# Round-robin block order in a blocked triangular inverse, one evacuation copy for four blocks, and partition sums on four column strips

## The chip, the cores and the metric

The kernel runs on one core of one Trainium2 chip. The metric is the device time of one execution in microseconds; three executions of the kernel before took 1111.55, 1113.08 and 1113.27 us, median 1113.08 us. TensorE (PE) multiplies, with its weight loads shown apart (PEld); VectorE (DVE), ScalarE (ACT) and GpSimd (POOL) work on vectors; SyncE (SP), ACT and POOL also issue transfers.

## The reference, cut to what matters

One layer of a diffusion backbone over 512 latent tokens and 256 context tokens, width 1024: a modulated norm, one combined input projection, two token mixers side by side (a gated delta rule with four heads and HGRN2 with four heads, each in both directions), an up-projection of each, a gated merge, an output projection and a SwiGLU. The change touches the delta rule's inverse and sums over partitions. In the reference the inverse is a triangular solve for each chunk:

```python
a_mat = jnp.where(strict, beta[..., :, None] * jnp.einsum('bhnid,bhnjd->bhnij', k, k) * decay, 0.0)
rhs = jnp.concatenate([(beta * jnp.exp(g))[..., None] * k, beta[..., None] * v], axis=-1)
sol = lax.linalg.triangular_solve(a_mat, rhs, left_side=True, lower=True, unit_diagonal=True)
...
m_lat = (jax.nn.silu(c) @ mod_w[layer] + mod_b[layer])[:, None, :]
...
return tf * lax.rsqrt(jnp.sum(tf * tf, axis=-1, keepdims=True) + EPS)
```

The last two lines are where sums over partitions come from: the six modulation sections, and the squared norms of queries and keys.

## The kernel before

Weights come in float32, are split into a high and a low part (L92 to L97: a load, an ACT cast `hi`, a DVE subtraction `lo`), and each projection is three products (`mm3`, L105) of 512 or 256 tokens. The mixers are streams: `G0` and `G2` are pairs of delta-rule heads (`gdn_pair`), `H0` to `H3` are HGRN2 heads (`hgrn`), `F` are gate projections used as filler. PLAN (L31) sets the order in which they are emitted; a list scheduler then merges them into one fixed order for each engine, by priority and its own estimates of durations. Each engine runs its list in order. After the delta rule (X in PLAN) its memory is freed, and the loads of the remaining modulation weights (`mwb`, POOL queue, L819) start; then come the up-projections (`pup`), the output projection (`pwo`) and the SwiGLU (`pf`, `pfo`).

The delta rule's inverse (L668 to L757) runs once for each pair of heads. The 128-token chunk is four diagonal 32 x 32 blocks, inverted on DVE (L680 to L685). Then two merging steps, each for e = 0, 1 (the heads of the pair), six chunks g and both directions d:

- 32 to 64: for four blocks (d, b) with rows a and columns z (`quads`), `pR` = N·X (L724), copied to SBUF by ACT (L727), then `pY` = R·Y (L730) and, for two of the blocks, `pX` (L733); ACT copies them into N and X64 (L737, L739).
- 64 to 128: the same with 64 x 64 blocks, two of them: `pRb` (L747), its copy (L750), `pYb` (L753), its copy (L756).

Each product occupies only the 32 x 32 or 64 x 64 block of the PE array that `tile_position` names. The matrices are float32, and the profile shows two PE passes (a weight load and a matmul each) for one such product: L724 has 96 products and 192 passes. All six products of a block are issued one after the other, then the next block.

A sum over partitions is a product of the data as weights [128, 128] with a column of ones: `pn` in `gdn_front` (L623, squared norms: six chunks for keys, four for queries, four heads) and `pmo` in `mod_sum` (L846, two for each of 16 quarter sections). The early modulation sums of `modulation` (L265) have the same form.

Of the kernel before, what the change touches and what calls it, by code (L numbers as in the profile page):

```python
# [13 lines left out]
P = 128  # L14
# [15 lines left out]
# The order in which the streams of the mixers are emitted: name and number of steps; X ends the delta rule.  # L30
# [13 lines left out]
def view(ap, offset, dims):  # L44
    """The tile behind ap, all partitions, with free dimensions given as (step, count)."""
    return bass.AP(ap.tensor, ap.offset + offset, [list(ap.ap[0])] + [list(d) for d in dims])


def body(tc, T, out, tap=None):
# [8 lines left out]
    with ExitStack() as root:  # L58
# [25 lines left out]
        def split(srcs, kt, n, pool=None):  # L84
            """Loads [kt * 128, n] of weights side by side and splits them into two float32r parts."""
            WN[0] += 1
            pool = pool or ring["w"]
            raw = pool.tile([P, kt, n], F32, name=f"raw{WN[0]}", tag="raw", bufs=2)
            c0 = 0
            for s in srcs:  # L90
                w = s.shape[1]
                nc.sync.dma_start(raw[:, :, c0:c0 + w], s.rearrange("(k p) f -> p k f", p=P))  # L92
                c0 += w
            hi = pool.tile([P, kt, n], F32R, name=f"hi{WN[0]}", tag="hi")
            nc.scalar.copy(hi[:, :, :], raw[:, :, :])  # L95
            lo = pool.tile([P, kt, n], F32R, name=f"lo{WN[0]}", tag="lo")
            nc.vector.tensor_tensor(lo[:, :, :], raw[:, :, :], hi.bitcast(F32), op=ALU.subtract)  # L97
            return hi, lo

        def mm3(ps, a, b, kt, start=True, stop=True):  # L100
            """ps += sum_k a_k^T b_k with a, b as (hi, lo) callables of k."""
# [5 lines left out]

        def feat(w, src, n, name, t0=0, tag="mm"):
            """[128 features, n tokens from t0] of the projection with the weights w."""
            ps = bank(tag, name)  # L110
            mm3(ps[:, 0:n], [lambda k, t=t: t[:, k, :] for t in w], [lambda k, t=t: t[:, k, t0:t0 + n] for t in src], KT)
            return ps
# [19 lines left out]
        def gate_low(i, pool):  # L132
            """The same in two halves of the features, out of its own buffers."""
# [15 lines left out]
        with ExitStack() as st:  # L149
# [4 lines left out]
            # small vectors, one row of 128 to a partition: those of the first norm, then the others  # L154
# [71 lines left out]
            def sigmoid_small(dst, src):  # L226
                """1 / (1 + exp(-src)), for the small tiles."""
# [25 lines left out]
            def modulation(d, s):  # L253
                """Shift and scale columns of feature tile d, for the latents (s = 0) or the context (s = 1)."""
# [12 lines left out]
            def mod_columns(s, d0, d1):  # L267
                """The columns of the feature tiles d0 to d1, with the biases and the weight of the norm."""
# [144 lines left out]
        def head_norm(po, gcol, i, on, y, ss, tag, name, eq=None):  # L413
            """po: [128 tokens, 4, 128] -> normalised, scaled by the channel weight, transposed, spilled as row i of ydram."""
# [15 lines left out]
        def hgrn(h):  # L430
            """HGRN2 head, both directions; index 0 of L is the backward one, of K and R the forward one."""
# [19 lines left out]
            for d in range(3):  # L451
# [7 lines left out]
                # softplus(-|z|), then the sigmoids of both signs  # L459
# [100 lines left out]
        def gdn_front(h, res):  # L560
            """Projections and convolution of a Gated DeltaNet head. Queries and keys stay as they are: the norms of the
            keys go into the write strengths and the values, those of the queries into the norm of the output."""
# [9 lines left out]
            for kind, c0 in (("k", 512), ("q", 0), ("v", 1024)):  # L572
# [46 lines left out]
                else:  # L619
                    nc.scalar.activation(acc[:, 0:P * cnt], flat, AF.Square)  # L620
                    pn = bank("ga", m + "pn")
                    for g in range(cnt):
                        nc.tensor.matmul(pn[:, g:g + 1], acc[:, P * g:P * g + P], ones[:, 0:1], start=True, stop=True)  # L623
# [11 lines left out]
        def gdn_pair(h0):  # L635
            """Two Gated DeltaNet heads, both directions."""
# [5 lines left out]
            # decay products and intra-chunk matrices  # L642
# [25 lines left out]
            # inverse of the unit-triangular matrices: 32 x 32 blocks, one block to a partition  # L668
# [40 lines left out]
            R1 = [t.rearrange("p (u c) -> p u c", c=32) for t in spare]  # L709
# [7 lines left out]
            for e in range(2):  # L717
# [3 lines left out]
                for d, b, a, z in quads:  # L721
                    for g in range(6):
                        u, o = 12 * d + 6 * e + g, 192 * d + 32 * g
                        nc.tensor.matmul(pR[z, o:o + 32], NU[a, u, z], Xd[d][a, u, :],  # L724
                                         start=True, stop=True, tile_position=(a.start, z.start))
                for d, b, a, z in quads:
                    nc.scalar.copy(R1[d][z, :, :], pR[z, 192 * d:192 * d + 192].rearrange(c6, c=32))  # L727
                    for g in range(6):
                        u, o = 12 * d + 6 * e + g, 192 * d + 32 * g
                        nc.tensor.matmul(pY[a, o:o + 32], R1[d][z, g, :], Yd[d][z, u, :],  # L730
                                         start=True, stop=True, tile_position=(z.start, a.start))
                        if b == d:
                            nc.tensor.matmul(pX[z, o:o + 32], Yd[d][z, u, :], R1[d][z, g, :],  # L733
                                             start=True, stop=True, tile_position=(z.start, z.start))
                for d, b, a, z in quads:
                    u6 = slice(12 * d + 6 * e, 12 * d + 6 * e + 6)
                    nc.scalar.copy(NU[a, u6, z], pY[a, 192 * d:192 * d + 192].rearrange(c6, c=32))  # L737
                    if b == d:
                        nc.scalar.copy(X64[z, 6 * e:6 * e + 6, 32 * d:32 * d + 32], pX[z, 192 * d:192 * d + 192].rearrange(c6, c=32))  # L739
                yield  # L740
            top, bot = slice(0, 64), slice(64, P)
            for e in range(2):
                pR = bank("ga", f"{n}pRb{e}")
                pY = bank("ga", f"{n}pYb{e}")
                for d, a, z in ((0, top, bot), (1, bot, top)):
                    for g in range(6):
# [4 lines left out]
                for d, a, z in ((0, top, bot), (1, bot, top)):  # L751
                    for g in range(6):
                        nc.tensor.matmul(pY[a, 64 * g:64 * g + 64], R2[g // 3][z, g % 3, :], NU[z, 12 * d + 6 * e + g, z],  # L753
                                         start=True, stop=True, tile_position=(z.start, a.start))
                    u = 12 * d + 6 * e
# [3 lines left out]
            # scan over the chunks, forward and backward  # L759
# [51 lines left out]
        def mod_quarter(sec, j):  # L811
            """Columns of a quarter of a section of the modulation, with the bias added."""
# [16 lines left out]
        def mod_early(sec, j, tag):  # L829
            """The same in the memory of a buffer of the delta rule that waits for its use, summed at once."""  # L830
# [12 lines left out]
        def mod_sum(sec, j, acc, tag):  # L843
            ps = bank(tag, f"pmo{sec}{j}")
            for i in range(2):
                nc.tensor.matmul(ps[:, i:i + 1], acc[:, P * i:P * i + P], ones[:, 0:1], start=True, stop=True)  # L846
# [5 lines left out]
        def mod_steps(n):  # L852
            """Each step multiplies a part of a quarter."""
# [4 lines left out]
        def mod_sums():  # L858
            """The sums over the partitions."""
# [3 lines left out]
        def row_bcast(dst, col, tag):  # L863
            """dst[p, 128 * j + i] <- col[i, j] on every partition."""
# [39 lines left out]
        # the delta rule is done: the rest of the modulation  # L904
# [26 lines left out]
        with pool("mg", 1) as mg:  # L931
# [3 lines left out]
            with pool("yp", 1) as yp:  # L935
                def branch(br):
                    """Gates the normalised outputs of a branch and splits them."""
# [14 lines left out]
                def up(br, W, ys):  # L952
                    """Up-projection of a branch, times its merge gate, summed over the branches."""
# [30 lines left out]
            # output projection, token-major, in two halves of the tokens; gated residual, second norm  # L984
# [132 lines left out]
```

## Time and profile before

| | |
|---|---|
| median of three executions | 1113.08 us (1111.55 to 1113.27) |
| span of the profiled execution | 1115.9 us |
| PE busy | 1054.0 us, 94% |
| PE weight loads busy | 879.1 us, 79% |
| DVE, ACT, POOL busy | 696.8, 560.1, 75.8 us |
| TensorE clock granted, mean | 0.980 |

The page gives for the profiled execution its span, from the first instruction to the last; that execution's own time is not given beside it. Its span is 2.8 us above the median of the timed ones. The PE share counts each matmul from its start to its modelled end, and matmuls overlap, so starts, not durations, tell how long PE is held.

### The profile page before, as it was taken

The numbers are of one execution on the slowest core, as the hardware profiler recorded it, in microseconds if no ns is written. First come the engines' busy times: TensorE is split into PE (matmuls) and PEld (weight loads), VectorE is DVE, ScalarE is ACT, GpSimd is POOL, SyncE is SP. The second block draws the span as 40 slices with busy tenths as digits, with TensorE's granted clock in tenths as the row PEclk, the third lists the DMA queues.
The fourth block names the chain that finished last, engine by engine and source line by source line (L and its number), as shares of the span: only waits on it lengthen the run. The fifth ranks groups of instructions, "written<-read, shape, count | busy, mean of one in ns | idle before, by whom it ended". The sixth has DMA issues, their size and how long they took to land.

```text
span 1115.9 us, 15740 instructions
## 1 busy us (share of the span) xinstructions
PE 1054.0 (94%) x6007; PEld 879.1 (79%) x6007; DVE 696.8 (62%) x1365; ACT 560.1 (50%) x1062; POOL 75.8 (7%) x132
## 2 busy tenths in 40 slices
PE   4999999979999999999988999899999999999996
PEld 3787788858897887799777887787888888888785
DVE  5896877679676868866796675586343433422424
ACT  3454568747886765887764743452222222221212
POOL 0010000220001022000201000010000000000000
PEclk9998999989999999999999999999999999999999
DMA  9943322222003213200637853455333332322222
GB/s 303 283 149 109 114 76 57 58 76 57 3 20 114 76 48 86 57 2 11 194 118 227 299 153 123 129 167 159 93 93 94 94 88 80 93 94 94 92 95 94
DMA packets 142720, 122.02 MB, mean 109 GB/s; under 512 B 5534, under 2 KB 118452, under 8 KB 142644
## 3 DMA queue, kind: packets, MB, share of 16 engines
q1 hardware_dynamic: 135907, 100.20, 30.1%
q0 software_dynamic: 4640, 17.30, 4.8%
q10 hardware_dynamic: 2096, 3.50, 1.0%
q8 instruction: 47, 0.77, 0.3%
q14 instruction: 30, 0.24, 0.1%
HBM read 110.51 MB, written 10.49 MB: 108 GB/s over the span
## 4 chain that ended last, share of the span: by engine, by line
PE 57%; DVE 10%; issue 5%; ACT 3%; POOL 2%; DMA 2%; POOLq 0%; ACTq 0%; DVEq 0%
PE pf L105 19%; PE pfo L105 10%; PE pgate L105 4%; PE pup L105 4%; PE pwo L105 3%; PE h_z L105 2%; DMA mwb<-in_mod_w_dram 2%; PE h_pA L477 2%; PE h_zv L105 1%; DVE lo L97 1%; PE p_s_pk L778 1%; PE p_s_pk L787 1%; DVE p_o L683 1%; PE p_s_pk L775 1%; DVE p_Z L685 1%
## 5 line engine op out<-in xcount | busy, mean ns | idle before, releaser
L95 ACT CAST hi<-raw 128x1024 fp32r<-128x1024 f32 (+1 forms) x137 | 135.7, 991 | 307.4 <-PE pf L105 131.2
L97 DVE TENSOR_TENSOR lo<-raw,hi 128x1024 fp32r<-128x1024 f32 (+1 forms) x137 | 157.9, 1152 | 177.5 <-ACT hi L95 176.9
L105 PE MATMUL pf<-hhi,lo 128*128 128x512 f32 (+1 forms) x368 | 142.9, 389 | 2.4 <-DVE lo L97 2.4
L105 PE MATMUL pf<-hlo,hi 128*128 128x512 f32 (+1 forms) x368 | 143.0, 390 | 0.7 <-DVE hlo L1030 0.7
L105 PE MATMUL pf<-hhi,hi 128*128 128x512 f32 (+1 forms) x368 | 142.4, 390 | 0.0
L105 PEld LDWEIGHTS pf<-hhi,lo 128*128 128x128 f32 x368 | 69.8, 190 | 18.5 <-DVE lo L97 3.3
L105 PEld LDWEIGHTS pf<-hlo,hi 128*128 128x128 f32 x368 | 69.7, 190 | 16.5 <-DVE hlo L1030 1.1
L105 PEld LDWEIGHTS pf<-hhi,hi 128*128 128x128 f32 x368 | 69.7, 190 | 15.1
L105 PE MATMUL pfo<-lo,uh 128*128 128x512 f32 x176 | 69.8, 396 | 0.1
L105 PE MATMUL pfo<-hi,ul 128*128 128x512 f32 x176 | 69.5, 395 | 0.0
L105 PE MATMUL pfo<-hi,uh 128*128 128x512 f32 x176 | 68.7, 395 | 0.0
L105 PE MATMUL pgate<-hhi,lo 128*128 128x512 f32 x144 | 60.6, 422 | 6.7 <-DVE lo L97 6.7
L105 PE MATMUL pgate<-hhi,hi 128*128 128x512 f32 x144 | 61.1, 424 | 1.8 <-ACT hi L95 1.8
L105 PE MATMUL pgate<-hlo,hi 128*128 128x512 f32 x144 | 59.8, 416 | 0.0
L1053 DVE TENSOR_TENSOR sg<-sg,pf 128x512 f32<-128x512 f32 x22 | 15.1, 688 | 53.2 <-PE pf L105 53.2
L821 DVE SCALAR_TENSOR_TENSOR acc<-mwb,sc,acc 128x256 f32<-128x256 f32 x72 | 34.3, 482 | 13.0 <-DMA mwb<-in_mod_w_dram 11.7
L261 DVE SCALAR_TENSOR_TENSOR macc<-mw,sc,macc 128x256 f32<-128x256 f32 x96 | 40.0, 479 | 0.0
L105 PEld LDWEIGHTS pfo<-lo,uh 128*128 128x128 f32 x176 | 33.1, 188 | 8.7 <-DVE lo L97 1.0
L105 PEld LDWEIGHTS pgate<-hhi,lo 128*128 128x128 f32 x144 | 28.5, 198 | 14.4 <-DVE lo L97 9.2
L105 PE MATMUL h_z<-hhi,hi 128*128 128x512 f32 x96 | 39.3, 410 | 0.3 <-ACT abT L365 0.3
L105 PE MATMUL h_z<-hlo,hi 128*128 128x512 f32 x96 | 39.4, 411 | 0.0
L105 PEld LDWEIGHTS pfo<-hi,uh 128*128 128x128 f32 x176 | 32.9, 188 | 8.2 <-ACT hi L95 0.6
(422 smaller groups left out, 2566.3 us busy)
## 6 DMA issues: line engine op xcount, KB each, us to landing
raw<-in_ffn_w_in_dram SPq DMA_DIRECT2D x44, 512.0 KB, 3.9
raw<-in_w_in_dram SPq DMA_DIRECT2D x37, 512.0 KB, 3.9
raw<-in_ffn_w_out_dram SPq DMA_DIRECT2D x22, 512.0 KB, 3.5
mwb<-in_mod_w_dram POOLq DMA_DIRECT2D x18, 512.0 KB, 4.9
mw<-in_mod_w_dram SPq DMA_DIRECT2D x16, 512.0 KB, 6.3
mwe<-in_mod_w_dram POOLq DMA_DIRECT2D x7, 1024.0 KB, 6.2
gdram<-gt SPq DMA_DIRECT2D x24, 256.0 KB, 2.4
raw<-in_w_in_dram SPq DMA_DIRECT2D x18, 256.0 KB, 3.0
```

The costliest lines, as they stand in the source:

```text
L95: nc.scalar.copy(hi[:, :, :], raw[:, :, :])
L97: nc.vector.tensor_tensor(lo[:, :, :], raw[:, :, :], hi.bitcast(F32), op=ALU.subtract)
L105: nc.tensor.matmul(ps, a[u](k), b[v](k), start=(start and n == 0), stop=(stop and n == tot - 1))
L261: nc.vector.scalar_tensor_tensor(acc[:, :], mws[d][:, k, :], col, acc[:, :], op0=ALU.mult, op1=ALU.add)
L477: nc.tensor.matmul(pA[:, P * c:P * c + P], kq[:, 0, P * c:P * c + P], kq[:, 1, P * c:P * c + P], start=True, stop=True)
L683: nc.vector.tensor_tensor(ov, Z[:, r + 1:32, r:r + 1].to_broadcast([P, 31 - r, r]), Z[:, r:r + 1, 0:r].to_broadcast([P, 31 - r, r]), op=AL ...
L685: nc.vector.tensor_tensor(Z[:, r + 1:32, 0:r], Z[:, r + 1:32, 0:r], ov, op=ALU.add)
L775: nc.tensor.matmul(pk[:, 0:P], KTt[:, g, :], S[t][:, :], start=True, stop=True)
L778: nc.tensor.matmul(pk[:, P:2 * P], N[:, d, e, g, :], rt[:, :], start=True, stop=True)
L787: nc.tensor.matmul(pk[:, 2 * P:3 * P], kend[:, :], u[:, :], start=True, stop=True)
L821: nc.vector.scalar_tensor_tensor(acc[:, :], mw[:, k - k0, :], sc[:, k:k + 1], acc[:, :], op0=ALU.mult, op1=ALU.add)
L1053: nc.vector.tensor_tensor(sg[:, :], sg[:, :], pgu[1][:, :], op=ALU.mult)
```

## The change

Three edits, with nothing else of the program's text changed but comments.

1. In the inverse the two loops are exchanged: for each chunk g the products of the four blocks (or of the two 64 x 64 blocks) follow each other, so that consecutive products lie in different blocks of the array. `pX` comes after all of `pY`.
2. All four blocks of `pR` lie in the same 192 columns, on their own 32 partitions each. One ACT copy of [128, 192] takes the place of four of [32, 192]; the intermediate of e = 0 and that of e = 1 have a buffer each. The copies of `pX` go to DVE.
3. `column_sums` takes the place of one [128, 128] x [128, 1] product by four of [128, 32] x [128, 1], one for each strip of 32 columns, in `pn` and in `mod_sum`. `modulation` keeps its form.

```diff
+        def column_sums(ps, c, a):
+            for j in range(0, P, 32):
+                nc.tensor.matmul(ps[j:j + 32, c:c + 1], a[:, j:j + 32], ones[:, 0:1], start=True, stop=True, tile_position=(0, j))
...
                     for g in range(cnt):
-                        nc.tensor.matmul(pn[:, g:g + 1], acc[:, P * g:P * g + P], ones[:, 0:1], start=True, stop=True)
+                        column_sums(pn, g, acc[:, P * g:P * g + P])
...
-                for d, b, a, z in quads:
-                    for g in range(6):
-                        u, o = 12 * d + 6 * e + g, 192 * d + 32 * g
-                        nc.tensor.matmul(pR[z, o:o + 32], NU[a, u, z], Xd[d][a, u, :],
+                for g in range(6):
+                    for d, b, a, z in quads:
+                        nc.tensor.matmul(pR[z, 32 * g:32 * g + 32], NU[a, 12 * d + 6 * e + g, z], Xd[d][a, 12 * d + 6 * e + g, :],
                                          start=True, stop=True, tile_position=(a.start, z.start))
-                for d, b, a, z in quads:
-                    nc.scalar.copy(R1[d][z, :, :], pR[z, 192 * d:192 * d + 192].rearrange(c6, c=32))
-                    for g in range(6):
-                        u, o = 12 * d + 6 * e + g, 192 * d + 32 * g
-                        nc.tensor.matmul(pY[a, o:o + 32], R1[d][z, g, :], Yd[d][z, u, :],
+                R1 = R1s[e]
+                nc.scalar.copy(R1[:, :, :], pR[:, 0:192].rearrange(c6, c=32))
+                for g in range(6):
+                    for d, b, a, z in quads:
+                        nc.tensor.matmul(pY[a, 32 * g:32 * g + 32], R1[z, g, :], Yd[d][z, 12 * d + 6 * e + g, :],
                                          start=True, stop=True, tile_position=(z.start, a.start))
+                for g in range(6):
+                    for d, b, a, z in quads:
                         if b == d:
-                            nc.tensor.matmul(pX[z, o:o + 32], Yd[d][z, u, :], R1[d][z, g, :],
+                            nc.tensor.matmul(pX[z, 32 * g:32 * g + 32], Yd[d][z, 12 * d + 6 * e + g, :], R1[z, g, :],
                                              start=True, stop=True, tile_position=(z.start, z.start))
...
-                        nc.scalar.copy(X64[z, 6 * e:6 * e + 6, 32 * d:32 * d + 32], pX[z, 192 * d:192 * d + 192].rearrange(c6, c=32))
+                        nc.vector.tensor_copy(X64[z, 6 * e:6 * e + 6, 32 * d:32 * d + 32], pX[z, 0:192].rearrange(c6, c=32))
...
-                for d, a, z in ((0, top, bot), (1, bot, top)):
-                    for g in range(6):
+                for g in range(6):
+                    for d, a, z in ((0, top, bot), (1, bot, top)):
                         nc.tensor.matmul(pR[z, 64 * g:64 * g + 64], NU[a, 12 * d + 6 * e + g, z], X64[a, 6 * e + g, :],
...
-                nc.tensor.matmul(ps[:, i:i + 1], acc[:, P * i:P * i + P], ones[:, 0:1], start=True, stop=True)
+                column_sums(ps, i, acc[:, P * i:P * i + P])
```

The scheduler orders the new program anew, and from the first `pn` on the streams stand in a slightly different order on every engine. Line numbers of the changed kernel are higher by 5 to 8.

ACT's list in the inverse of the first pair, before: `p_T` is the SBUF intermediate, `p_pR`, `p_pY` and `p_pX` the PSUM banks, `h_E` and `h_kq` belong to the HGRN2 head that runs beside it.

```order
L727 COPY p_T_2358<-p_pR_2382 32x192 x2
L727 COPY p_T_2359<-p_pR_2382 32x192 x2
L500 ACTIVATE h_E_3217<-h_L 128x2x64x4
L501 ACTIVATE h_kq_3216<-h_K,lno 128x2x64x4
L737 COPY p_N<-p_pY_2383 32x6x32
L739 COPY p_X_2362<-p_pX_2384 32x6x32
```

The same place of the changed kernel:

```order
L732 COPY p_T_2472<-p_pR_2496 128x192
L505 ACTIVATE h_E_3331<-h_L 128x2x64x4
L506 ACTIVATE h_kq_3330<-h_K,lno 128x2x64x4
L744 COPY p_N<-p_pY_2497 32x6x32 x4
L506 ACTIVATE h_kq_3343<-h_K,lno 128x2x32x8
L732 COPY p_T_2473<-p_pR_2667 128x192
```

Four copies of `p_pR` have become one, and the copies of `p_pX` have left ACT. On DVE they now stand between steps of the HGRN2 head:

```order
L509 TENSOR_TENSOR h_K<-h_K,h_L 128x2x64x4
L746 COPY p_X_2476<-p_pX_2498 32x6x32 x2
L510 TENSOR_TENSOR h_L<-h_L 128x2x64x4
L487 COPY_PREDICATED h_AT<-lev,h_pA_3335 128x512
L509 TENSOR_TENSOR h_K<-h_K,h_L 128x2x32x8
L746 COPY p_X_2476<-p_pX_2669 32x6x32 x2
```

Behind the first pair of these copies DVE has `h_L` and `h_AT` queued. On PE the `pYb` products of the first pair's first head stood in two pieces, one for each direction, with the next `pRb` and an HGRN2 product (`h_pA`) between them:

```order
L753 MATMUL p_pYb_2771<-p_N,p_T_2358 64x64 x3
L753 MATMUL p_pYb_2771<-p_N,p_T_2359 64x64 x3
L747 MATMUL p_pRb_2800<-p_X_2362,p_N 64x64 x12
L477 MATMUL h_pA_3247<-h_kq_3242 128x128
L753 MATMUL p_pYb_2771<-p_N,p_T_2358 64x64 x3
L753 MATMUL p_pYb_2771<-p_N,p_T_2359 64x64 x3
```

In the changed kernel they stand together:

```order
L105 MATMUL g_k_zc<-clo,hi_3676 128x256
L760 MATMUL p_pYb_2885<-p_N,p_T_2472 64x64 x6
L760 MATMUL p_pYb_2885<-p_N,p_T_2473 64x64 x6
L754 MATMUL p_pRb_2914<-p_X_2476,p_N 64x64 x12
L482 MATMUL h_pA_3348<-h_kq_3343 128x128 x3
```

So two stays in the 64 x 64 form have become one, and its consecutive products now alternate between the two directions' blocks.

## Rows read from the trace of the kernel before

**Rows 1.** The page: the chain that ended last, shares of the span by engine.
```profile
PE 57%; DVE 10%; issue 5%; ACT 3%; POOL 2%; DMA 2%; POOLq 0%; ACTq 0%; DVEq 0%
```
**Rows 2.** Stretches: us, PE, PEld, DVE, ACT, POOL busy, clock, DMA share, GB/s.
```profile
100.00:545.00 445.00, 423.75 (x3116) 367.42 (x3116) 335.26 (x725) 313.32 (x691) 49.79 (x87) 0.98 0.21 61
280.00:303.00 23.00, 21.43 (x399) 19.02 (x398) 15.94 (x23) 20.06 (x50) 0.74 (x1) 1.00 0.01 2
```
**Rows 3.** The chain that ended last, second pair's inverse: start us, us, what.
```profile
469.66 1.60 PE p_pR L724 x48
```
**Rows 4.** The same chain in the first pair's inverse.
```profile
286.80 0.31 ACT p_T L727
...
295.56 0.32 ACT p_X L739
```
**Rows 5.** Timeline, PE around the first pair's first pR: start us, us, what.
```profile
282.43 1.40 PE L724 MATMUL p_pR<-p_T,p_N 32*32 32x32 f32 x48 [1.37 <-DVE p_T L692]
...
283.76 0.50 PE L105 MATMUL g_k_zl<-hlo,hi 128*128 128x512 f32 x1
```
**Rows 6.** Timeline, PE passes of pY, pX and the next pR.
```profile
287.42 0.19 PE L730 MATMUL p_pY<-p_T 32*32 32x32 f32 x1
...
287.64 0.19 PE L730 MATMUL p_pY<-p_T 32*32 32x32 f32 x1
...
288.55 0.19 PE L730 MATMUL p_pY<-p_T 32*32 32x32 f32 x1
...
288.56 0.19 PE L724 MATMUL p_pR<-p_T,p_N 32*32 32x32 f32 x1
...
288.56 0.19 PE L733 MATMUL p_pX<-p_T 32*32 32x32 f32 x1
```
**Rows 7.** Timeline, PE passes with 64 x 64 blocks.
```profile
293.20 1.43 PE L747 MATMUL p_pRb<-p_X,p_N 64*64 64x64 f32 x24
...
294.56 1.16 PE L477 MATMUL h_pA<-h_kq 128*128 128x128 f32 x8
...
298.56 0.91 PE L753 MATMUL p_pYb<-p_N,p_T 64*64 64x64 f32 x12
...
299.40 0.94 PE L477 MATMUL h_pA<-h_kq 128*128 128x128 f32 x6
```
**Rows 8.** Timeline, PE from whole-array products into 64 x 64 blocks.
```profile
484.33 0.28 PE L105 MATMUL h_z<-clo,hi 128*128 128x256 f32 x1
484.45 0.28 PE L105 MATMUL h_z<-chi,lo 128*128 128x256 f32 x1
484.66 0.73 PE L753 MATMUL p_pYb<-p_N,p_T 64*64 64x64 f32 x9
```
**Rows 9.** Timeline, PE around a sum over partitions.
```profile
140.21 1.40 PE L623 MATMUL g_k_pn<-ones,g_k_acc 128*128 128x1 f32 x12
141.47 0.49 PE L105 MATMUL pgate<-hhi,lo 128*128 128x512 f32 x1
```
**Rows 10.** Groups of the sums: xcount, busy us, mean ns of one, idle before.
```profile
L623 PE MATMUL g_k_pn<-ones,g_k_acc 128*128 128x1 f32 x48 | 5.7, 245 | 0.0
L846 PE MATMUL pmo<-ones,acc 128*128 128x1 f32 x36 | 4.5, 237 | 0.1
L623 PE MATMUL g_q_pn<-ones,g_q_acc 128*128 128x1 f32 x32 | 4.1, 249 | 1.9 <-ACT g_q_acc L620 1.9
L846 PE MATMUL pmo<-ones,mwe 128*128 128x1 f32 x28 | 3.7, 237 | 2.6 <-DVE mwe L840 2.6
```
**Rows 11.** Groups of copies and of one DVE operation, by line.
```profile
L727 ACT COPY p_T<-p_pR 32x192 f32<-32x192 f32 x16 | 5.0, 310 | 0.4
L750 ACT COPY p_T<-p_pRb 128x192 f32<-128x192 f32 x8 | 2.3, 322 | 1.6 <-PE p_pYb L753 1.5
L802 DVE TENSOR_TENSOR p_oa<-p_oa,p_s_pk 128x128 f32<-128x128 f32 x32 | 8.8, 284 | 4.4 <-ACT p_oa L801 4.2
```
**Rows 12.** The chain behind the end of the delta rule.
```profile
544.74 7.74 DMA mwb<-in_mod_w_dram
```

More of the change, by code (lines that the diff above doesn't have):

```diff
@@ L708, in gdn_pair @@
             spare = [t[:, 24:32, :].rearrange("p u c -> p (u c)")[:, 0:192] for t in (T1, T2)]
-            R1 = [t.rearrange("p (u c) -> p u c", c=32) for t in spare]
+            R1s = [t.rearrange("p (u c) -> p u c", c=32) for t in spare]
             R2 = [t.rearrange("p (u c) -> p u c", c=64) for t in spare]
@@ L736, in gdn_pair @@
                     u6 = slice(12 * d + 6 * e, 12 * d + 6 * e + 6)
-                    nc.scalar.copy(NU[a, u6, z], pY[a, 192 * d:192 * d + 192].rearrange(c6, c=32))
+                    nc.scalar.copy(NU[a, u6, z], pY[a, 0:192].rearrange(c6, c=32))
                     if b == d:
-                        nc.scalar.copy(X64[z, 6 * e:6 * e + 6, 32 * d:32 * d + 32], pX[z, 192 * d:192 * d + 192].rearrange(c6, c=32))
+                        nc.vector.tensor_copy(X64[z, 6 * e:6 * e + 6, 32 * d:32 * d + 32], pX[z, 0:192].rearrange(c6, c=32))
                 yield
@@ L750, in gdn_pair @@
                     nc.scalar.copy(R2[i], pR[:, 192 * i:192 * i + 192].rearrange(c6, c=64))
-                for d, a, z in ((0, top, bot), (1, bot, top)):
-                    for g in range(6):
+                for g in range(6):
+                    for d, a, z in ((0, top, bot), (1, bot, top)):
                         nc.tensor.matmul(pY[a, 64 * g:64 * g + 64], R2[g // 3][z, g % 3, :], NU[z, 12 * d + 6 * e + g, z],
                                          start=True, stop=True, tile_position=(z.start, a.start))
+                for d, a, z in ((0, top, bot), (1, bot, top)):
                     u = 12 * d + 6 * e
```

## The prediction

> **What bounds the kernel now.** I read the chain of waits by engine first: PE carries 57% of the span, DVE 10%, nothing else over 5% [rows 1]. Then busy time by stretch: in the mixers, from 100 to 545 us, PE is busy 424 of 445 us, DVE 335 and ACT 313 [rows 2]. Nearly all that the change touches lies there. PE is the limit, but a busy PE says little by itself, since matmuls overlap in the record; so I looked at starts in the timeline, and at who carries the chain in the two inverses. In the second pair's it is PE itself: the 48 passes of `pR` stand there whole, 1.60 us [rows 3]. In the first pair's it is ACT without a break from 286.80 to 295.88 us: eight R copies, eight Y copies, four X copies and four activations of the HGRN2 head [rows 4]; ACT is busy 20.1 of 23 us there, PE 21.4 [rows 2]. So in one inverse a PE pass saved is time saved, in the other an ACT copy saved.
>
> **Inverse, 32 x 32 blocks.** Within one block a pass starts every 31.7 ns: `pY` goes from 287.42 to 287.64 in seven steps [rows 6]. But three blocks run abreast near 288.56: a `pY`, a `pR` and a `pX` pass start within 0.01 us, each block still keeping its own pace [rows 6]. So it is the block that is slow, not the array, and going round the blocks pays. Three starts per 31.7 ns, 10.6 ns each, is the densest issue that the trace shows; four blocks need 7.9 ns. I price at 10.6 and keep 7.9 as the better end.
> - `pR`: 282.43 to the next whole-array product at 283.76 is 1.33 us for 48 passes [rows 5]. The last pass starts at 282.43 + 1.40 - 0.19 = 283.64, so 0.12 us is the way out. After: 48 x 0.0106 + 0.12 = 0.63, saving 0.70.
> - `pY` and `pX`: 72 passes, of which the second starts at 287.42 and the last but one or two at 288.56 [rows 6], so 1.2 us. `pX` now comes last, in two blocks only: 48 x 0.0106 + 12 x 0.0317 = 0.89, saving 0.31.
> - `pRb`: 24 passes of two blocks one after the other, 293.20 to 294.56, 1.36 us; 12 passes of one block with both switches, 298.56 to 299.40, 0.84 [rows 7]. Two blocks abreast should cost 0.84 plus a little: 0.9, saving 0.46.
> - `pYb`: two stays of 0.84 become one of 0.9, saving 0.78.
>
> That is 2.25 us for each e, four times: 9.0 us of PE. At 7.9 ns it would be 9.0 + 4 x (48 + 48) x 0.0027 = 10.0.
>
> The Trainium skill has a rule against this: in "TensorEngine Tiling (Array Packing)", Restrictions and Gotchas, different row tiles cannot access one PSUM bank at the same time, and all four blocks of `pR` share a bank. The trace contradicts it as far as the time goes: in the 48 passes of `pR` each next block starts before the block ahead has ended, else 48 x 31.7 ns would be 1.52 us and not the 1.21 measured from first to last start [rows 5]. It stays as the slow rival below.
>
> **ACT copies.** One of 128 x 192 took 322 ns, one of 32 x 192 310 [rows 11]: partitions are free. Each e loses three R copies and two X copies, 5 x 0.31 = 1.55 us; a pair loses 3.1, and in the first pair that is the chain. The single copy must wait for all four blocks, where the first used to wait for one; but four blocks now end together at about 0.5 us, and the first PE pass behind it waited for its copy anyway. The new buffer for e = 1 takes away a wait on e = 0's `pY`, worth nothing on PE's list as it stands.
>
> **X copies on DVE.** The trace has no such copy. Nearest: a 128 x 128 operation reading PSUM, 284 ns [rows 11]; eight copies, 2.3 us in all. DVE has room (15.9 of 23 us) [rows 2], so from below the price is nothing, and from above 2.3 us plus the wait for `pX`, during which `h_L` and `h_AT` of the HGRN2 head are held, and behind them ACT's `h_E` and `h_kq` and the `h_pA` products. PE has filler then. I take 1 us.
>
> **Sums over partitions.** 48 + 32 + 36 + 28 = 144 passes [rows 10], each holding PE 0.1117 us: twelve lead from 140.21 to 141.47, the first a little shorter [rows 9]. That is 16.0 us. After: 576 passes with 32 columns of weights. No row shows four strips under all 128 rows. Nearest are `pY` and `pX` of one quad: they read the same 32 partitions, write different strips, and run abreast [rows 6]. At 10.6 ns it is 6.1 us, at 7.9 ns 4.6, one after the other at 31.7 ns 18.3. Against that stand switches of form: the way out above costs 0.12 us where the next pass would cost 0.03, and the way in, 484.45 to 484.66, 0.21 where such a product holds PE 0.12 [rows 8]. Some 0.2 us, for 19 separate groups (24 groups, a few adjacent): 3.8 us. Net: 16.0 - 6.1 - 3.8 = 6.1 saved; between 7.6 saved and 6.1 lost. I take 6.1, since the abreast pair is the nearer row.
>
> **The sum.** Of the PE savings I count: the second pair's inverse in full, 4.5; the first pair's by its ACT chain, 3.1; the sums by PE's share of the chain, 0.57 x 6.1 = 3.5. Off that 1 for DVE and 1 for the new order of the streams, whose cost can have either sign. That is 9.1 us: span 1115.9 - 9.1 = 1106.8. The profiled span is 2.8 above the median of the timed runs, so 1113.1 - 9.1 = 1104.0. What is gained before 545 us is not swallowed there: the next transfer of modulation weights starts at 544.74 only when the delta rule's memory is free [rows 12], and moves with it.
>
> **Rivals.**
> - *Issue-bound.* PE may take one float32 product (two passes) per 31.7 ns, as in `pY`/`pX`. Then `pR` saves 0.45, `pY`/`pX` nothing, the 64 x 64 steps their 1.24: 6.8 in all. The strips take 288 x 0.0317 + 3.8 = 12.9 and save 3.1. Chain: 3.4 + 3.1 + 1.8 - 2 = 6.3, so 1107. For it: no row has more than three abreast, and those only for a few passes out of what was queued. The Trainium skill, "TensorE: Matmul & The Clock Gate", Part 1, gives about 25 ns as the least distance between matmul starts; the rows show 5 to 10 between blocks. Taken for whole products (two passes) it would give about 1105.
> - *Given back.* The freed PE time turns into waits on DVE and POOL in the streams (DVE has 10% of the chain [rows 1]), or the new order loses what was won: within 2 us of before, 1112. For it: ACT and DVE are each over 70% busy there; against it: PE hardly idles, 21 of 445 us [rows 2].
> - *Slower: turns.* If passes into one bank take turns, `pR` becomes 1.52 (0.3 more), `pY`/`pX` 72 x 0.0317 = 2.28 (1.08 more), so 5.5 us more over four; the strips lose 6.1. PE is held 11.6 us longer; 57% of it, less 3.1 on ACT, is 3.5, and up to 8 if PE carries it all: 1117 to 1121, say 1118. It decides where the strips' passes come more than 21 ns apart ((16.0 - 3.8) / 576).
>
> **Chances.** Forecast 0.58 (own range 1099 to 1109), issue-bound 0.20, given back 0.12, turns or a worse order 0.10. A measurement of this kernel can tell 0.2%, 2.2 us, from no change. Faster takes the first two and a quarter of the third, 0.81; same 0.09; slower 0.10. Range: below, the forecast with 7.9 ns and all PE savings on the path, 10.0 + 7.6 - 1 = 16.6, gives 1096.5; above, to the given-back case: 1097 to 1112.
>
> **What the changed profile would show.** `pR`'s 48 passes in about 0.5 us and four names abreast; `pn`'s 48 passes in about 0.5 to 0.6 us before the way out; four R copies of 128 x 192 on ACT in place of 16; the first pair's inverse, from its first `pR` to its last `pYb`, three to five us shorter. I would be wrong if strip passes come 30 ns apart, if DVE holds the X copies until PE runs out of filler, or if the stretch from 100 to 545 us is as long as before.

## The result and the profile after

The changed kernel takes 1098.64 us (median of 4 runs, 1098.47 to 1099.97) against 1112.32 us before (4 runs, 1111.55 to 1113.27): a ratio of 0.9886, 95% interval 0.9871 to 0.9901, 13.7 us less. Forecast were 1104.0 us, 9.1 us less; the time lies inside the range and 0.4 us under the forecast's own range. Timed again in a later session, the same two kernels gave 0.9896 (0.9869 to 0.9923), 11.6 us less.

The page of the changed kernel: busy time of the engines, and the chain by engine, which answers to [rows 1] (PE there 57%).

```profile
PE 1034.3 (94%) x6439; PEld 856.0 (78%) x6439; DVE 699.2 (64%) x1373; ACT 554.6 (50%) x1042; POOL 75.7 (7%) x132
...
PE 70%; DVE 12%; ACT 6%; issue 5%; DMA 4%; POOL 3%; SPq 0%; POOLq 0%; ACTq 0%; DVEq 0%
```

PE was busy 1054.0 us of 1115.9 before and 1034.3 of 1098.3 now. So its idle time stayed (61.9 and 64.0 us), and the whole gain is PE busy time.

Windows of the changed kernel, in the columns of [rows 2]; the second and third are the two inverses, from the first `pR` to the last `pYb`.

```profile
100.00:545.00 445.00, 420.35 (x3498) 358.60 (x3499) 348.25 (x751) 318.93 (x687) 51.84 (x89) 0.99 0.23 67
277.50:292.50 15.00, 13.41 (x378) 11.43 (x379) 11.48 (x21) 14.07 (x34) 0.74 (x1) 1.00 0.01 4
463.50:477.50 14.00, 12.37 (x369) 10.72 (x369) 10.01 (x19) 13.28 (x32) 0.74 (x1) 1.00 0.01 4
```

The same two stretches of the kernel before:

```profile
282.40:303.40 21.00, 20.77 (x400) 18.80 (x400) 13.68 (x21) 18.53 (x47) 0.74 (x1) 1.00 0.01 4
469.60:491.40 21.80, 21.74 (x389) 19.12 (x389) 11.07 (x18) 18.15 (x46) 0.74 (x1) 0.92 0.01 2
```

PE idled 0.2 and 0.1 us inside the two inverses before, and idles 1.5 us inside each now, waiting for ACT's copies of R before `pY` and of `pRb` before `pYb`.

By the starts in the timelines the first pair's inverse went from 20.8 to 14.6 us and the second's from 21.7 to 13.7. In either, 9.2 us are now left up to the first `pRb` (10.8 and 12.0 before), and 5.4 and 4.5 from there to the last `pYb` (10.0 and 9.8 before).

Timeline of PE in the changed kernel: a sum over partitions (against [rows 9]), `pR` (against [rows 5]), and the 64 x 64 step (against [rows 7]).

```profile
140.22 0.40 PE L105 MATMUL pgate<-hlo,hi 128*128 128x512 f32 x1
140.54 0.58 PE L111 MATMUL g_k_pn<-ones,g_k_acc 128*32 128x1 f32 x48
141.05 0.51 PE L105 MATMUL g_k_zl<-hhi,hi 128*128 128x512 f32 x1
141.39 0.40 PE L105 MATMUL g_k_zl<-hlo,hi 128*128 128x512 f32 x1
...
277.59 0.62 PE L729 MATMUL p_pR<-p_T,p_N 32*32 32x32 f32 x48 [1.31 <-DVE p_T L697]
278.14 0.50 PE L105 MATMUL g_k_zl<-hlo,hi 128*128 128x512 f32 x1
...
286.81 0.92 PE L754 MATMUL p_pRb<-p_X,p_N 64*64 64x64 f32 x24
287.65 0.39 PE L105 MATMUL g_k_zc<-clo,hi 128*128 128x256 f32 x1
...
289.09 0.92 PE L760 MATMUL p_pYb<-p_N,p_T 64*64 64x64 f32 x24 [0.34 <-ACT p_T L757]
289.84 0.87 PE L754 MATMUL p_pRb<-p_X,p_N 64*64 64x64 f32 x24
```

The 48 passes of `pR` now lie within 0.62 us. Less the last pass's own 0.19 that is 0.43 from first to last start, where it was 1.21: 9 ns a pass, four blocks abreast. The next product follows `pR` after 0.55 us; it was 1.33. `pRb` holds PE for 0.84 us (1.36 before). `pYb` of both directions holds it for 0.75, with no gap before the next `pRb`, where two stays of 0.84 were. The sum of 48 passes holds it for 0.51 us; with 0.09 more on the way in (0.32 from start to start, where wide products follow at 0.23) and 0.11 more on the way out, 0.71 in place of 1.26 (140.21 to 141.47 in [rows 9]) and 0.09 on the way out, 1.35. The way out was there before the change too, since the product after the sum held PE for 0.32 us:

```profile
141.47 0.49 PE L105 MATMUL pgate<-hhi,lo 128*128 128x512 f32 x1
141.79 0.39 PE L105 MATMUL pgate<-hhi,hi 128*128 128x512 f32 x1
```

Counted in this way over both traces (from the first start of a group to the start of the next other product, less idle time), the sums hold PE for 15.2 us before and 7.5 now, and the products of the inverse for 22.3 and 12.4.

Pieces of the chain that ended last in the changed kernel, the first four in the first pair's inverse, the others in the second pair's.

```profile
281.95 0.33 ACT p_T L732
...
285.47 0.32 ACT p_T L732
...
288.72 0.33 ACT p_T L757
...
289.09 0.92 PE p_pYb L760 x24
...
471.41 0.33 ACT p_T L732
...
471.78 0.70 PE p_pY L735 x47
472.48 0.39 PE p_pX L740 x24
472.87 0.84 PE p_pRb L754 x24
```

ACT still carries the first pair's chain up to the 64 x 64 step (against [rows 4]). In the second pair PE carries it from the second head's `pY` on; ahead of that it is ACT now, where PE carried it before (against [rows 3]). The groups of copies in the changed kernel, against [rows 11]:

```profile
L732 ACT COPY p_T<-p_pR 128x192 f32<-128x192 f32 x4 | 1.3, 318 | 0.1
L744 ACT COPY p_N<-p_pY 32x192 f32<-32x192 f32 x16 | 4.9, 306 | 0.1
L746 DVE COPY p_X<-p_pX 32x192 f32<-32x192 f32 x8 | 2.8, 353 | 0.2
```

**One sum for all traces.** A span is PE's idle time, plus what a lowered clock costs, plus the rest. Idle is the span less PE's busy time on the page. For the clock I took windows of 2 us through the whole span and added (1 - granted clock) x PE busy of each. The rest is called work at full clock here. It is worked out, not read off; four traces of the same products in much the same order (the changed kernel twice, X on ACT twice) give 1020.8 to 1023.7, so differences of up to 3 us say nothing. The clock column is the mean granted clock over the timed runs.

| kernel | span | idle | slow clock | work | clock (runs) | ratio, 95% |
|---|---|---|---|---|---|---|
| before | 1115.9 | 61.9 | 19.2 | 1034.8 | 0.983 (49) | 1 |
| changed | 1098.3 | 64.0 | 13.5 | 1020.8 | 0.986 (4) | 0.9886 (0.9871-0.9901) |
| changed, again | 1100.5 | 65.1 | 13.2 | 1022.2 | 0.985 (6) | 0.9896 (0.9869-0.9923) |
| sums alone | 1113.7 | 63.7 | 20.0 | 1030.0 | 0.981 (12) | 0.9983 (0.9964-1.0002) |
| inverse alone | 1105.6 | 61.8 | 15.3 | 1028.5 | 0.986 (6) | 0.9927 (0.9907-0.9946) |
| 64 x 64 step alone | 1112.2 | 64.4 | 16.6 | 1031.2 | 0.982 (12) | 0.9986 (0.9967-1.0004) |
| 32 x 32 step alone | 1122.9 | 66.7 | 24.0 | 1032.2 | 0.976 (6) | 1.0105 (1.0065-1.0145) |
| block by block | 1105.7 | 62.3 | 10.9 | 1032.5 | 0.985 (12) | 0.9963 (0.9948-0.9978) |
| four copies of R | 1106.5 | 65.5 | 19.4 | 1021.6 | 0.982 (6) | 0.9936 (0.9913-0.9958) |
| X on ACT | 1094.0 | 62.7 | 10.3 | 1021.0 | 0.988 (5) | 0.9865 (0.9840-0.9890) |
| X on ACT, again | 1093.7 | 63.8 | 6.2 | 1023.7 | 0.988 (4) | 0.9868 (0.9848-0.9888) |
| and more sums on strips | 1089.9 | 64.9 | 8.6 | 1016.4 | 0.988 (4) | 0.9837 (0.9817-0.9856) |
| more passes, pair 0 | 1123.7 | 77.6 | 18.4 | 1027.7 | 0.975 (4) | 1.0140 (1.0118-1.0163) |
| more passes, pair 1 | 1122.9 | 77.0 | 19.1 | 1026.8 | 0.971 (5) | 1.0157 (1.0141-1.0173) |

From before to changed: work -14.0, slow clock -5.7, idle +2.1, together the 17.6 us between the two spans. The timed runs differ by less, 13.7 us. A span is 1.7 us shorter than the time of its execution wherever both are on record, so the profiled execution of before was some 5.3 us slower than the median of its four timed runs, and that of the changed kernel 1.3 us slower than its own.

### The profile page after: what moved, and what is told of

It reads as the page before. It is cut to its first block, busy times and chain, and to the rows that moved or that the text cites. A ratio compares the mean times of both kernels' runs of the same rounds, so it can differ in the third digit from the quotient of the medians.

```text
span 1098.3 us, 16604 instructions
## 1 busy us (share of the span) xinstructions
PE 1034.3 (94%) x6439; PEld 856.0 (78%) x6439; DVE 699.2 (64%) x1373; ACT 554.6 (50%) x1042; POOL 75.7 (7%) x132
## 4 chain that ended last, share of the span: by engine, by line
PE 70%; DVE 12%; ACT 6%; issue 5%; DMA 4%; POOL 3%; SPq 0%; POOLq 0%; ACTq 0%; DVEq 0%
PE pf L105 22%; PE pfo L105 10%; PE pgate L105 5%; PE pup L105 4%; PE pg L316 3%; PE h_z L105 3%; PE pwo L105 3%; DVE lo L97 2%; PE h_zv L105 2%; PE p_s_pk L795 1%; PE pmod L270 1%; PE h_pA L482 1%; PE g_k_zl L105 1%; PE p_s_pk L786 1%; DMA mwb<-in_mod_w_dram 1%
## 5 line engine op out<-in xcount | busy, mean ns | idle before, releaser
L105 PEld LDWEIGHTS pf<-hlo,hi 128*128 128x128 f32 x368 | 70.1, 191 | 15.3 <-DVE hlo L1038 0.5
L1061 DVE TENSOR_TENSOR sg<-sg,pf 128x512 f32<-128x512 f32 x22 | 15.1, 687 | 51.6 <-PE pf L105 51.5
L105 PEld LDWEIGHTS pfo<-hi,ul 128*128 128x128 f32 x176 | 33.2, 188 | 7.6
```

Of the source, the lines that this page charges most:

```text
L105: nc.tensor.matmul(ps, a[u](k), b[v](k), start=(start and n == 0), stop=(stop and n == tot - 1))
L1061: nc.vector.tensor_tensor(sg[:, :], sg[:, :], pgu[1][:, :], op=ALU.mult)
```

## The experiments

Four theories stood against each other. A: the products abreast and the missing copies pay by the prediction's terms. B: the order of the 64 x 64 step pays, since `pYb` of one direction no longer stands behind products of other streams. C: what the sums gain is given back at the next wait. D: part of the gain is the clock of those runs.

**The sums alone** (kernel before, `column_sums` in `gdn_front` and `mod_sum`).

```
-  nc.tensor.matmul(pn[:, g:g + 1], acc[:, P * g:P * g + P], ones[:, 0:1], start=True, stop=True)
+  column_sums(pn, g, acc[:, P * g:P * g + P])
```

> The kernel before with the column sums alone on four strips; the inverse is as before. Theory A (the prediction's terms hold, each part pays by its passes): 3.5 us, a ratio near 0.997. Rival C (what the sums gain before 350 us is given back at the next wait on data, as the marks of the changed kernel hint, where 11.7 us of lead at 336 us are 4.5 us at 353 us): under 1 us, a ratio of 0.999 to 1.000.

Ratio 0.9983 (0.9964 to 1.0002), 1.9 us less: it can't be told from no change, and sits between A and C. The trace has A's work, 1030.0 against 1034.8, so 4.8 us less; from the first `k_pn` to the first `pD`, where PE idles about 1 us, the time goes from 52.8 to 49.8 us. Its runs had a mean clock of 0.981 where before's had 0.983. Through its runs, as through those of the 64 x 64 step alone and of block by block, 0.01 of clock goes with 9 to 10 us (7 through 29 of before's; lines through the 4 to 11 runs of the others scatter from 3 to 14). So its slightly lower clock hides some 2 us of the gain.

**The inverse alone** (the changed kernel with the sums above turned back).

> The changed kernel with the sums over partitions as 128x1 products again; the whole change of the inverse stays. Theory A: the rest of the 13.7 us, about 10 us, a ratio near 0.991. Rival C: nearly all of it, 13 us, a ratio near 0.988. In the trace the inverse takes 14 to 15 us in either pair of heads under both.

Ratio 0.9927 (0.9907 to 0.9946), 8.2 us less: A's 10 us is inside the interval, C's 13 us is not. C falls: beside the rest the sums are worth what is missing here, 4.6 us against the first timing of the changed kernel and 3.4 against the second, whose interval overlaps this one. Why the lead shrinks between 336 and 353 us isn't shown.

**The 64 x 64 step alone.**

```
-  for d, a, z in ((0, top, bot), (1, bot, top)):
-      for g in range(6):
+  for g in range(6):
+      for d, a, z in ((0, top, bot), (1, bot, top)):
           nc.tensor.matmul(pY[a, 64 * g:64 * g + 64], ...)
-      nc.scalar.copy(NU[a, u:u + 6, z], ...)
+  for d, a, z in ((0, top, bot), (1, bot, top)):
+      nc.scalar.copy(NU[a, u:u + 6, z], ...)
```

The loops of `pRb` are turned in the same way.

> The kernel before with the change in the 64x64 step of the inverse alone (both directions go by turns for pRb and pYb, and the copies of pYb follow the products of both). Theory A (overlapped passes pay): 0.46 + 0.78 us for each of four heads, 5 us at the most and 3 to 4 on the path, a ratio of 0.996 to 0.997. Rival B (the order pays: pYb of one direction no longer stands behind the first copy and behind products of other streams): 8 to 10 us, a ratio of 0.991 to 0.993, and from the first pRb to the end of pYb 5 us instead of 10 in the trace.

Ratio 0.9986 (0.9967 to 1.0004), 1.6 us less, which can't be told from no change; work is 3.6 us less, within A's 3 to 4. B falls: from the first `pRb` to the end of `pYb` the trace shows 6.3 us where 10.0 and 9.8 were, and yet the time hardly moves. Fewer products of other streams stand in the stretch now. They stand elsewhere.

**Block by block** (the changed kernel with its copies where they are, loops turned).

```
-  for g in range(6):
-      for d, b, a, z in quads:
+  for d, b, a, z in quads:
+      for g in range(6):
           nc.tensor.matmul(pR[z, 32 * g:32 * g + 32], ...)
```

and so for `pY`, `pX`, `pRb`, `pYb`.

> The changed kernel with its copies where they are (behind the products of all blocks, one copy of R, X on the vector engine), but with the products emitted block by block again, so that no two blocks of the array run abreast. The sums stay on strips. Theory A (the overlap pays): the 9 us of passes come back, 6 to 9 us of it on the path, a ratio near 0.994 to 0.996 against the kernel before. Rival B (the places of the copies pay, the overlap little): 0.989 to 0.991, within 3 us of the changed kernel; the step from pRb to pYb then stays below 7 us.

Ratio 0.9963 (0.9948 to 0.9978), at the upper end of A's range. Timeline of PE in this kernel, and below it part 1 of its page:

```profile
277.55 1.40 PE L729 MATMUL p_pR<-p_T,p_N 32*32 32x32 f32 x48 [1.33 <-DVE p_T L697]
278.88 0.50 PE L105 MATMUL g_k_zl<-hlo,hi 128*128 128x512 f32 x1
...
288.60 1.43 PE L754 MATMUL p_pRb<-p_X,p_N 64*64 64x64 f32 x24
...
290.99 1.43 PE L760 MATMUL p_pYb<-p_N,p_T 64*64 64x64 f32 x24
```
```profile
PE 1043.4 (94%) x6439; PEld 865.3 (78%) x6439; DVE 699.8 (63%) x1373; ACT 554.9 (50%) x1042; POOL 75.7 (7%) x132
```

The same 6439 passes, `pR` back at 1.33 us, and PE's work 11.7 us above the changed kernel's; by the starts the inverse's products hold PE for 23.1 us. Going round the blocks is worth 7.5 us or so of time (0.9896 against 0.9963, intervals apart); without it the rest of the inverse's edit shows no gain clear of the noise beside the sums alone (0.9963 against 0.9983). That PE is the faster for it answers the rule quoted in the prediction: the Trainium skill, "TensorEngine Tiling (Array Packing)", Restrictions and Gotchas, says that different row tiles can't access one PSUM bank at the same time. Here four row tiles write one bank, each its own 32 partitions, 48 passes in 0.43 us against 1.21 one block after the other. The measurement decides.

**The changed kernel again**, beside the three that follow.

> The changed kernel as it is, timed on the same chip as the three kernels beside it, with the granted clock of each of its runs. Theory A (the gain is passes and copies): a ratio of 0.986 to 0.989 again. Rival D (a part of the 13.7 us came from runs in which the granted clock happened to stay high, 0.983 to 0.987 over the run): a ratio of 0.989 to 0.993, and at an equal mean clock the gain is near 11.5 us, what the sums alone and the inverse alone gave together at a clock of 0.984 (4.3 and 7.2 us, read off the lines through their runs).

Ratio 0.9896 (0.9869 to 0.9923), 11.6 us less, mean clock 0.985: between A and D. Six runs can't part the two. By the lines above, 0.002 to 0.003 more clock are 1.5 to 3 us. With work -12.6 to -14.0 and idle +2.1 to +3.2 from the two traces, the time without the clock is 9.4 to 12.0 us less.

**The 32 x 32 step alone** (kernel before with the round-robin `pR`, `pY`, `pX`, one R copy, X on DVE).

> The kernel before with the change in the 32x32 step of the inverse alone (round-robin products, one copy of R for four, X on the vector engine); the 64x64 step and the sums as before. Theory A: passes (0.70 + 0.31 us for each of four heads, 4.0 us) and copies on the first pair's chain (3.1 us), less 1 us for the vector engine: 4 to 6 us, a ratio of 0.9945 to 0.9965. Rival B (the 64x64 step's order carries the gain of the inverse): under 3 us, 0.9975 or more. In the trace the step from the first pR to pRb takes 9.2 us in both pairs by A.

Ratio 1.0105 (1.0065 to 1.0145): slower by 13.4 us, which no theory had. The step itself is 9.2 and 9.6 us long, as A said, and work is 2.6 us less. Windows and timeline of this kernel at the second pair's 64 x 64 step, which here goes one block after the other, as before:

```profile
480.00:484.00 4.00, 3.31 (x135) 2.82 (x133) 2.04 (x5) 3.89 (x11) 0.00 (x0) 1.00 0.01 4
484.00:488.00 4.00, 3.08 (x98) 2.83 (x99) 3.69 (x7) 3.45 (x9) 0.00 (x0) 0.93 0.01 4
488.00:492.00 4.00, 4.00 (x39) 3.78 (x39) 2.42 (x5) 1.48 (x4) 0.00 (x0) 0.50 0.00 0
...
500.00:504.00 4.00, 4.00 (x24) 3.77 (x24) 0.91 (x3) 1.90 (x5) 0.00 (x0) 0.50 0.00 0
```
```profile
486.13 1.46 PE L754 MATMUL p_pRb<-p_X,p_N 64*64 64x64 f32 x24
...
488.32 0.41 PE L105 MATMUL h_z<-chi,lo 128*128 128x256 f32 x1
488.53 0.41 PE L105 MATMUL h_z<-chi,hi 128*128 128x256 f32 x1
...
493.32 1.54 PE L760 MATMUL p_pYb<-p_N,p_T 64*64 64x64 f32 x12
```

From 487 to 504 us the granted clock is 0.50, that is 1.2 GHz, all through the split `pYb` and the start of the scan. Twelve `pYb` passes take 1.54 us there, 0.91 at 2.4 GHz [rows 7]; 128x256 products follow each other at 0.21 us, not 0.12 [rows 8]. Before it fell, PE had idled 1.6 of the 8 us from 480 and run small products. The runs' mean clock, 0.976 (four of six at 0.969 to 0.975), makes some 6 us of the 13.4. Of the rest the trace shows 4.8 us as idle time, 3.1 of it between the first scan and the second pair's `pD`. Why the clock falls here for so long, and why each half alone gives little or loses while both together gain 8.2 us, stays open.

**X on ACT** (the changed kernel, run twice on two occasions).

```
-  nc.vector.tensor_copy(X64[z, 6 * e:6 * e + 6, 32 * d:32 * d + 32], ...)
+  nc.scalar.copy(X64[z, 6 * e:6 * e + 6, 32 * d:32 * d + 32], ...)
```

> The changed kernel with the copies of X on the scalar engine again (two of 0.31 us for each head; on the vector engine they take 0.354 us). Theory A (in the first pair the scalar engine is the chain of the 32x32 step): 0.6 to 1.2 us longer from pR to pRb in the first pair, nothing in the second, the time 0.1% above the changed kernel's or less. Rival E (the vector engine's queue is what delays X64 and with it pRb): no longer or shorter by up to 1 us.

> The changed kernel with the X copies on the scalar engine once more, beside the candidate. If the 2.5 us against the changed kernel were real: a ratio of 0.9855 to 0.9875. If they were a matter of the granted clock (0.988 in the mean of its runs against 0.985): 0.987 to 0.990, with a mean clock near 0.985.

Ratios 0.9865 (0.9840 to 0.9890) and 0.9868 (0.9848 to 0.9888), 2 to 3 us better than the changed kernel, with intervals that overlap its own. `pR` to `pRb` is 9.1 us for 9.2, as rival E has it, but that is too little to carry the gain, and the step from `pRb` on is 0.7 to 0.9 us longer; work is the same. The traces differ in the slow clock (10.3 and 6.2 us against 13.5 and 13.2) and by 0.2 to 2.4 us of idle time. The mean clock was 0.988 on both occasions, and the second ratio lies where a real gain was put (0.9855 to 0.9875); what in the order keeps the clock up isn't shown.

**Four copies of R** (the changed kernel, one copy per block).

```
-  nc.scalar.copy(R1[:, :, :], pR[:, 0:192].rearrange(c6, c=32))
+  for d, b, a, z in quads:
+      nc.scalar.copy(R1[z, :, :], pR[z, 0:192].rearrange(c6, c=32))
```

> The changed kernel with four copies of R, one for each block, in the place of the one that takes all four (three more of 0.31 us for each head on the scalar engine); the products stay as they are. Theory A (copies pay where the scalar engine is the chain, that is in the first pair): pR to pRb 1.9 us longer in the first pair and up to as much in the second, 2 to 3 us in all, a ratio 0.002 to 0.003 above the changed kernel's. Rival F (the copies hide behind products of other streams): no change within 1 us, since the tensor engine is busy through the stretch in either case.

Ratio 0.9936 (0.9913 to 0.9958), 3.9 us above the changed kernel beside it; the intervals just overlap. `pR` to `pRb` is 1.8 us longer in the first pair, as A said, and 3.6 in the second, where 3.4 us of it ran at 1.2 GHz. But work is the same (1021.6), idle 0.4 us more, and PE idles less inside the inverses (0.6 and 1.2 us): copies lengthen the step, and other streams' products fill it. The loss of this trace is slow clock, 6 us more. The slow stretches that the changed kernel lacks lie at 424, 458, 526 to 537, 560 and 905 us, only that at 458 in an inverse. So it isn't shown that the copies bring them about, and neither A nor F is settled by the time.

**More passes in one pair** (the changed kernel; `h0 == 2` in the second kernel). The products write columns of `pX`'s bank that nobody reads.

```
+  for x in range(48 if h0 == 0 else 0):
+      g = x % 6
+      for d, b, a, z in quads:
+          nc.tensor.matmul(pX[z, 192 + 32 * g:224 + 32 * g], R1[z, g, :], Yd[d][z, ...], ...)
```

> The changed kernel with products added that nobody reads, in the first pair of heads alone: behind pX, 192 more 32x32 products for each of its two heads, on the four blocks by turns, into unused columns of pX's bank; 384 passes at 7.9 ns are 3.0 us a head, 6.1 us in all. The prediction's step (in the first pair the scalar engine is the chain, so passes of the tensor engine hide there): 0 to 2 us, a ratio of 0.989 to 0.991. Rival G (the tensor engine is the bound through the whole stretch, other streams' products fill every wait, so that a pass counts wherever it stands): the whole 6 us, a ratio of 0.994 to 0.996, and in the trace the tensor engine's work at full clock 6 us more, its idle time the same.

> The same added products in the second pair of heads alone. The prediction's step (there the tensor engine is the chain) and rival G agree here: 6 us, a ratio of 0.994 to 0.996.

Ratios 1.0140 (1.0118 to 1.0163) and 1.0157 (1.0141 to 1.0173), 27 and 29 us above the changed kernel: no theory had that. The timeline of the first of them, at a pause in the first head's train of added passes, and below it the group of half of the added passes, with its idle time and what ended that:

```profile
289.40 0.19 PE L745 MATMUL p_pX<-p_T,p_T 32*32 32x32 f32 x1
291.77 0.25 PE L745 MATMUL p_pX<-p_T,p_T 32*32 32x32 f32 x1 [2.18 <-issue]
```
```profile
L745 PE MATMUL p_pX<-p_T,p_T 32*32 32x32 f32 x384 | 10.6, 221 | 8.2 <-issue 8.2
```

Every 128 passes PE stops for 0.5 to 2.6 us with nothing to wait for but issue, and the clock falls to 1.2 GHz (290 to 310 us in the first kernel). Work rises by 5 to 6 us in either kernel, as rival G has it, idle by 12 to 14 and slow clock by 5 to 6. So the test of the price of a pass was spoilt by a supply of instructions that ran dry (see the last section). `pR` to `pRb` grew by 19.9 us in the first pair and by 22.5 in the second, and the spans by 22 to 25. That is far more than a wait for ACT in either pair could cover, so it doesn't tell whether a few passes would have been hidden in the first pair.

**More sums on strips** (X on ACT, and the first modulation's sums too).

```
-  nc.tensor.matmul(pmod0[:, c:c + 1], acc[:, P * j:P * j + P], ones[:, 0:1], start=(i == 0), stop=(i == 1))
+  column_sums(pmod0, c, acc[:, P * j:P * j + P], i == 0, i == 1)
```

> A candidate to beat the changed kernel: its X copies on the scalar engine again (1099.0 against 1101.6 us when the two ran side by side), and the 64 sums over partitions of the first modulation also on four column strips. Theory A (work of the tensor engine is what counts): 64 sums of about 0.06 us less are up to 4 us, but they stand in the first 110 us, where the tensor engine idles 20 us and waits for transfers: 0 to 2 us better than the X copies alone, a ratio of 0.985 to 0.987. Rival: each switch of the array's form costs about 0.2 us, the sums stand between wide products one by one, and the time is up to 3 us worse, 0.987 to 0.990.

Ratio 0.9837 (0.9817 to 0.9856), 1094.1 us: faster than before by 17.8 us and, with its interval apart, than the changed kernel (0.9886). It is 3.3 us faster than X on ACT beside it, where A said 0 to 2, but those two intervals overlap. The groups of X on ACT alone, then of this kernel:

```profile
L270 PE MATMUL pmod<-ones,macc 128*128 128x1 f32 x128 | 16.6, 248 | 5.7 <-DVE macc L266 5.7
```
```profile
L111 PE MATMUL pmod<-ones,macc 128*32 128x1 f32 x512 | 8.7, 176 | 8.4 <-DVE macc L266 8.3
```

Busy time falls by 7.9 us, and 2.7 come back as a longer wait for DVE. Work is 4.6 to 7.3 us less than in the two traces of X on ACT. So the idle time there hides a part of the saving, not all of it.

## Why the prediction was right, and where it was short

- **Abreast.** Right, at its better end. `pR` 0.55 us (forecast 0.63), `pRb` 0.84 (0.9), `pYb` 0.75 to 0.84 (0.9); `pY` with `pX` 0.97 and 1.02 up to the start of `pRb` (0.89), the one that fell short. By the starts the inverse's products hold PE 9.9 us less (22.3 to 12.4), where 9.0 was forecast and 10.0 was the better end; in work it is 6.3 (inverse alone) to 9.2 (all less the sums alone).
- **Sums.** 6.1 us forecast; in work 4.8 (sums alone) and 6.3 to 7.7 (changed less inverse alone). The sizes behind it were off and offset each other. The 144 passes held PE for 15.2 us, not 16.0, because the first of each group is shorter than the rest, and the 576 hold it for 7.5, not 6.1. Against that, of the 0.2 us for switching the 0.1 on the way out was paid before too; only the 0.1 on the way in is new. So 7.7 us less of holding and some 2 us of switches leave some 5.7. A group of twelve passes gains 0.64 us; a group of four goes from 0.37 to 0.24 and pays most of that back on the way in.
- **The discount for the path.** PE's savings of 15.1 us were cut to 4.5 for the second pair, 3.1 for the first "by its ACT chain" and 0.57 of the sums, 11.1 us, less 2. In the two traces 14.0 and 12.6 us of work go, and idle time takes back 2.1 and 3.2: 12.0 and 9.4 are left, so the forecast's 9.1 lies just below the lower of the two. What failed is the difference between the pairs. The prediction let all PE time count in the second pair and only ACT copies in the first. By the starts each pair's products hold PE 4.9 to 5.0 us less, and in each new idle time takes some of it back, 1.3 us in the first and 1.5 in the second, at waits for ACT's copies. That is 3.6 us net in the first (3.1 put) and 3.5 in the second (4.5 put). Before the change PE was busy 21.4 of 23 us beside the first pair's chain of ACT [rows 2], so there too a pass saved let other streams' products move up; and in the second pair, once PE is faster, the copies that ACT still makes carry the chain. The two misses nearly cancel, which is luck.
- **X on DVE.** 353 ns, not 284. X on ACT is 2 to 3 us faster, but work is the same and most of the difference is slow clock, so the 1 us is neither shown nor refuted.
- **New order, 1 us.** It can't be told by itself: idle time is up by 2.1 us in all, and the two inverses alone add 2.8.
- **The clock** was not a term at all. It gives 1.5 to 3 us between the two kernels' runs, and so a good part of the 4.6 us (2.5 in the second timing) by which the gain exceeds the forecast. How much of the rest is real, these runs can't tell.
- **Rivals.** Issue-bound falls for bursts of 48 to 72 passes (9 ns a pass). In trains of 384 another limit shows, the supply of instructions. Given back falls: 11.6 to 13.7 us stay. Turns (forecast 1118) falls with block by block: with turns, going round the blocks could not be 7.5 us the faster.

## What to carry to other kernels

Where PE is busy nine tenths of the time in every stretch and other streams can fill its waits, price a change by the PE time that it removes, wherever the chain of waits points, and take off the waits that it opens: here 9.9 us less of holding in the inverses opened 2.8 us of waits for the copies between the products. Make small products abreast by emitting them round the blocks, in bursts of some tens of passes (trains of 384 stalled). And look at the granted clock of each variant's runs before an effect under 1% is put down to the edit.

## What the runs showed of the hardware

- Four 32 x 32 blocks of one PSUM bank, each with its own partitions, and four 128-row strips run abreast: 9 ns a pass, where one block alone takes 31.7.
- A train of small passes outruns its instructions. In the first kernel with more passes the pauses come 128 passes apart, 2.18 us at 291.77. The profile has an instruction queue, q8, that moved 47 packets in the kernel before, with 6007 passes, and 56 here, with 7207: one packet for each 128 passes. The lines of the two pages:

```profile
q8 instruction: 47, 0.77, 0.3%
q8 instruction: 56, 0.92, 0.3%
```

In the trace the packets of q8 start at 285.68, 289.37, 296.73, 300.57 and 304.00 us, and PE goes on after its five pauses at 288.32, 291.77, 299.43, 302.89 and 306.34, each 2.3 to 2.7 us behind a packet's start. So each pause ends when the next block of instructions is there. The Trainium skill, "Runtime: NRT & Kernel Launch", Instruction fetch mechanics, says that engines refill their instruction memory in blocks of 256 instructions and that this is mostly hidden. A pass is a weight load and a product, so 128 passes are one such block, as the packets show; hidden it is not here.
- The clock fell once behind idle time followed by small products. Windows of the kernel before:

```profile
466.00:470.00 4.00, 2.46 (x25) 1.81 (x25) 4.00 (x3) 2.27 (x5) 0.28 (x1) 1.00 0.33 98
470.00:474.00 4.00, 4.00 (x50) 3.35 (x48) 1.45 (x3) 3.93 (x9) 0.47 (x1) 0.58 0.00 0
```

There PE idled 1.54 us, ran `pR` for 1.60 [rows 3], and from 470 to 474 us the granted clock was 0.58, partly at 1.2 GHz. In the changed kernel the same wait is followed by 0.43 us of `pR`, and 464 to 480 us stay at 1.00. But the shorter burst can't be the whole reason. Block by block has the wait and the long `pR` (1.33 us) at the same place, and its clock stayed up:

```profile
466.00:470.00 4.00, 2.53 (x54) 1.98 (x52) 3.90 (x5) 2.76 (x6) 0.74 (x1) 1.00 0.00 0
470.00:474.00 4.00, 4.00 (x37) 3.29 (x34) 0.67 (x1) 3.92 (x9) 0.00 (x0) 1.00 0.00 0
```

What decides it stays open.
